# Turning the 16 by 16 corners of the attention probabilities on VectorE instead of TensorE

## The chip, the cores and the metric

The kernel runs on 1 core of a Trainium2 chip. The metric is the device time of one execution in microseconds; it is the median of several runs. Beside it stands one execution recorded by the hardware profiler. The engines are named as the profile names them: PE is TensorE's matmul, PEld its weight load, DVE is VectorE, ACT is ScalarE, POOL is GpSimd, SP is SyncE, whose queue issues nearly all transfers.

## The reference

Two layers of a decoder trunk run over 528 positions: 16 learned meta tokens and 512 real ones, 1024 wide. Each layer normalises, projects into two groups of heads, concatenates their outputs, projects back, adds, and runs a SwiGLU feed-forward block of 2816. The part that the change touches is the first head group, 8 heads of forgetting attention (FoX) of 64 columns:

```python
def attend(q_blk, c_q, q_pos, k_, v_, c_k, k_pos):
    s = jnp.einsum('bhqd,bhkd->bhqk', q_blk, k_).astype(jnp.float32) * scale
    s = s + c_q[..., :, None] - c_k[..., None, :]
    s = jnp.where(k_pos[None, :] <= q_pos[:, None], s, -jnp.inf)
    p = jax.nn.softmax(s, axis=-1)
    return jnp.einsum('bhqk,bhkd->bhqd', p.astype(v_.dtype), v_)
```

The 16 meta queries are a block of their own; the 512 real queries go in 4 blocks of 128. The other group, 4 heads of retention (RetNet), is computed chunk by chunk and is not changed. After the second layer the meta rows are dropped.

## The kernel before

All activations are held transposed, features in partitions and positions in columns. Every product is made of numbers that are split into a high and a low part (`split`, lines 126 to 128: ScalarE copies the high part into a rounded format, VectorE subtracts it from the source for the low part), and a dense product is three matmuls per weight tile (`dense_steps`, L200). The weights come through SyncE's queue as `raw` tiles and are split into `whi` and `wlo` (L176, L177).

The FoX heads go in pairs: group g (0 to 3) holds heads 2g and 2g+1, called s = 0 and 1. `fox_steps` makes the list of steps of one group. For each head and each query block b, with b = -1 for the meta queries (first layer only) and b = 0 to 3 for the real ones, there are two steps:

- `scores(s, b)` multiplies keys and queries (L487) into a PSUM tile `psa`, of which there are four, adds the mask (L493), and lets VectorE write negated logits into a probability tile and take the minimum of a row (L494, `nmax`; block 3 has two halves whose minima are joined at L499). ScalarE then exponentiates in place and sums the rows (L507). The probability tile of b = 0 to 3 is `p_tiles[b]` (in the profile `pdNone`), of 128 x 128(b+2) columns, of which the last 112 hold zeros set once per layer; that of the meta block is one of two 128 x 128 `pm` tiles.
- `turn(s, b)` stands three steps later. It turns the block's probabilities through TensorE, 128 x 128 at a time with the identity `idt` as moving operand (`transpose_into`, L398), into PSUM, up to four in one bank, and splits each bank into `pth` and `ptl`, 128 keys x 5 key blocks x 528 queries.

A query block of 128 sees 16 + 128(b+1) keys, so its last key block holds only 16 keys, and these are visible only to the block's last 16 queries: a corner of 16 by 16.

`product(s)` multiplies the values with `pth` and `ptl` (L541 for the meta queries, L549 for the rest): key block j is used for the queries from column 128 j on. After the second head of a group the rows are scaled by the reciprocals of the sums (`rows`, L512, L514, L558, L559) and split into the mix tiles `mxh`, `mxl`.

TensorE's order is the program's: `merge` and `spread` place the steps of attention and retention between the chunks of the dense products by hand. The orders of the other engines are made by a scheduler from the same program; `high_priority` moves a piece forward and `pin` keeps one in its place. `layer` (from L1207) writes out which steps lie beside which dense products: groups 0 and 1 beside the retention projections and the next group's projections, group 2 beside half of the output projection (`add_h`, L760, adds it to the residual `h`), group 3 beside retention heads 2 and 3 and the other half.

Two early uses share the names of the probability tiles: the forget gates' weights are split into a tile tagged `pth` (`gate_weights`, L346 to L348), and the first layer's first value projection keeps its weights in a tile tagged `ptl` (`own`, L441 to L443).

Of the kernel before, what the change touches and what calls it, by code (L numbers as in the profile page):

```python
# [16 lines left out]
NK = D // 128  # L17
# [15 lines left out]
GAMMA = tuple(1.0 - 2.0 ** (-5 - h) for h in range(RH))  # L33
NEG = -1.0e30
HALF = T // 2


@with_exitstack
def hybrid_kernel(ctx, tc, x_t, w_in, w_fl, w_out, w_gate, w_up, w_down, vecs, b_fg, rope, decay, mask, ident, out_t):
# [23 lines left out]
    onec = const.tile([128, 1], F32, name="onec")  # L63
    nc.vector.memset(onec, 1.0)

    p_tiles, pm_tiles, v_tiles, end_tiles, low_keys = [], [], [], [], []
    rot = {"pm": 0}


# [10 lines left out]
    def enter_att(l):  # L80
        enter("att")
        low_keys[:] = [phase["att"].tile([128, T], F32R, name=f"kl{s}") for s in range(2)]
        for s, t in enumerate(low_keys):
            (nc.gpsimd if l else nc.vector).memset(t[64 * (1 - s):64 * (2 - s)].bitcast(F32), 0.0)

        for lst, n, cols, z0 in ((p_tiles, NBLK, None, None), (v_tiles, 2, TP, T)):
            lst[:] = [phase["att"].tile([128, cols or 128 * (i + 2)], F32, name=f"pd{z0}_{i}") for i in range(n)]
            for i, t in enumerate(lst):
                z = META + 128 * (i + 1) if z0 is None else z0
                zero(l, t[:, z:z + 128 - META])  # L90
        pm_tiles[:] = [phase["att"].tile([128, 128], F32, name=f"pm{i}") for i in range(2)] if l == 0 else []
        for t in pm_tiles:
            zero(l, t)
        end_tiles[:] = [[phase["att"].tile([128, META], F32R, name=f"rs{i}{k}") for k in range(2)] for i in range(2)]
        for t in end_tiles[0] + end_tiles[1]:
            zero(l, t.bitcast(F32))

    def zero(l, t):
        (nc.gpsimd if l else nc.vector).memset(t, 0.0)
# [50 lines left out]
    def convert(j, upto=NK, pinned=False):  # L150

        if j >= len(jobs):
            return
        job = jobs[j]
        fetch(j)
        if "make" in job:
            if "w" not in job:
                n = job["n"]
                hi, lo = (wring(job["ring"] + p) for p in ("whi", "wlo"))
                job["w"] = [(NK, hi, lo)]  # L160
                job["make"](hi[:, 0:n], lo[:, 0:n])
            return
        n = job["src"].shape[1]
        if "w" not in job:
            job["w"] = [(NK, *(job["own"]() if job["own"] else
                               [wp.tile([128, NK, 128], F32R, name=i, tag=i) for i in ("whi", "wlo")]))]
            job["split"] = 0
        sub = nc.gpsimd.tensor_sub if job["pool"] else nc.vector.tensor_sub
        while job["split"] < min(n, upto):
            c0 = job["split"]  # L170
            c1 = min(n, c0 + (2 if j < 2 and c0 < 4 else 4))
            size, hi, lo = job["w"][c0 // job["w"][0][0]]
            o = c0 % size
            hi, lo = hi[:, o:o + c1 - c0], lo[:, o:o + c1 - c0]
            with tc.high_priority() if j == 5 else ExitStack():
                pin(nc.scalar.copy(hi, job["raw"][:, c0:c1]), pinned)  # L176
            pin(sub(lo, job["raw"][:, c0:c1], hi.bitcast(F32)), pinned)  # L177
            job["split"] = c1
# [74 lines left out]
    def at(tag, dt=F32R, shape=(128, T), bufs=None):  # L253
        return phase["att"].tile(list(shape), dt, name=tag, tag=tag, bufs=bufs)
# [88 lines left out]
        nc.sync.dma_start(st["wfr"], w_fl[l])  # L343

    def gate_weights(l, st, pinned=False):
        wf = st["wf"] = at("pth", shape=(128, NK, 128))  # L346
        nc.gpsimd.memset(wf.bitcast(F32), 0.0)
        split(wf[:, :, 0:FH], wf[:, :, 32:32 + FH], st["wfr"], pinned)  # L348

    def forget_gates(l, st):  # L350
        if l:
            load_gates(l, st)
            gate_weights(l, st)
        else:
            for t, src in ((bfg, b_fg), (msk, mask), (idt, ident)):
                nc.sync.dma_start(t, src)
        wf = st["wf"]
        psf = [psum_a() for _ in FULL]
        for i in range(2 * NK):
            k, part = i // 2, i % 2  # L360
            for ps, (c0, c1) in zip(psf, FULL):
                nc.tensor.matmul(ps[:, 0:c1 - c0], wf[:, k, :], st["x"][k][part][:, c0:c1],
                                 start=(i == 0), stop=(i == 2 * NK - 1))
        z = tt("z")[0:FH]
        z2 = tt("z2")[0:FH]
        for ps, (c0, c1) in zip(psf, FULL):
            with ExitStack() if l else tc.high_priority():
                nc.scalar.copy(z2[:, c0:c1], ps[32:32 + FH, 0:c1 - c0])
                nc.vector.tensor_add(z[:, c0:c1], ps[0:FH, 0:c1 - c0], z2[:, c0:c1])
        st["z"] = z  # L370
# [31 lines left out]
    def fox_dense(l, g, ly, real, st):  # L402

        QC = REAL if real else FULL
        first = l + g == 0


        def q_done(ps):
            tq = tt("tq")
            with tc.high_priority() if first else ExitStack():  # L410
                nc.vector.scalar_tensor_tensor(sv(tq, real), pv(ps, real), RSC / 8.0, sv(ly["R"], real), ALU.mult, ALU.mult)
            st["q"] = []
            for s in range(2):
                t = at(f"qs{s}")
                a0, a1 = ROWS[s]
                b0, b1 = ROWS[1 - s]
                nc.scalar.copy(sv(t, real, a0, a1), sv(tq, real, a0, a1))
                nc.vector.tensor_sub(sv(t, real, b0, b1), sv(tq, real, a0, a1), sv(t, real, a0, a1).bitcast(F32))
                st["q"].append(t)


        def k_done(ps):
            tk = tt("tq")
            nc.vector.scalar_tensor_tensor(sv(tk, False), pv(ps, False), RSC, sv(ly["R"], False), ALU.mult, ALU.mult)
            st["k"] = []
            for s in range(2):
                kh = at(f"kh{s}")
                kl = low_keys[s]
                a0, a1 = ROWS[s]
                for b0, b1 in (ROWS[s], ROWS[1 - s]):  # L430
                    nc.scalar.copy(kh[b0:b1, :], tk[a0:a1, :])
                nc.vector.tensor_sub(kl[a0:a1, :], tk[a0:a1, :], kh[a0:a1, :].bitcast(F32))
                st["k"].append((kh, kl))

        def v_done(ps):
            vt = v_tiles[0]
            for t, (c0, c1) in zip(ps, FULL):
                nc.vector.scalar_tensor_tensor(vt[:, c0:c1], t[:, 0:c1 - c0], RSC, ly["R"][:, c0:c1],
                                               ALU.mult, ALU.mult)
            st["vt"] = vt  # L440

        def own():
            t = at("ptl", shape=(128, 2, NK, 128))  # L443
            return t[:, 0], t[:, 1]

        return [dense_steps(w_in[l, 3 * g + i], [(0, lambda k: ly["x"][k], NK, c, f)], g > 0 or (i == 2 and not first), i == 2,
                            ((), (6, 6))[i] if first and i < 2 else (1, 4), own if first and i == 2 else None, ly["wait"] if first and i < 2 else None)
                for i, (c, f) in enumerate(((QC, q_done), (FULL, k_done), (FULL, v_done)))]

    def fox_steps(g, st, ly, real):  # L450
# [21 lines left out]
        def scores(s, b):  # L472
# [5 lines left out]
                st["bc"] = bc  # L478
            bc = st["bc"]
            segs = FULL if nk == T else ((0, nk),)  # L480
            pt = take(pm_tiles, "pm") if b < 0 else p_tiles[b]
            mins = []
            normalise()
            for c0, c1 in segs:
# [21 lines left out]
            pr = pt[0:nq, 0:nk]  # L506
            nc.scalar.activation(pr, pr, AF.Exp, bias=nmax[0:nq], scale=-1.0, accum_out=rsum)  # L507
            info[s, b] = pt
            if b < 0:
                info["open"] = (pr, rsum)  # L510
            elif (s, b) == todo[-1]:
                nc.vector.reciprocal(st["sums"], st["sums"])  # L512
                st["rows"] = tt("tq")
                nc.scalar.copy(st["rows"][:, 0:SEQ].rearrange("p (b s d) -> p b s d", b=NBLK, s=2),  # L514
                               st["sums"].unsqueeze(3).broadcast_to([128, NBLK, 2, 64]))
# [6 lines left out]

        def turn(s, b):
            nq, nk, q0 = span(b)
            if b == blocks[0]:
                st["pt"] = (at("pth", shape=(128, 5, T)), at("ptl", shape=(128, 5, T)))
            pth, ptl = st["pt"]
            if (s, b) == todo[-2]:
                normalise()
            for j0, n, p3 in transpose_into(info[s, b], [128 * j for j in range(b + 2)]):  # L530
                split(pth[:, j0:j0 + n, q0:q0 + nq], ptl[:, j0:j0 + n, q0:q0 + nq], p3[:, :, 0:nq])

        def product(s):
            mt, v, pt = st["mt"], st["v"][s], st["pt"]
            a0, a1 = ROWS[s]
            b0, b1 = ROWS[1 - s]
            ol = tt("ol")
# [847 lines left out]
```

## Time and profile before

| | us |
| --- | --- |
| median of 3 runs | 1283.06 (1282.85 to 1283.12) |
| the profiled execution, time | 1283.16 |
| the profiled execution, span | 1281.3 |
| first layer, attention part, by the chain | about 0 to 283 |
| feed-forward of the first layer | about 283 to 652 |
| second layer, attention part | about 652 to 905 |
| feed-forward of the second layer, end | about 905 to 1281 |

The page of the profile gives busy times and shares per engine, then the chain that ended last: from the last instruction back, at each step, to what released it. The view of groups has rows of the form "line engine operation out<-in shape xcount | busy us, mean ns of one | idle time just before them and who ended it". The timeline and the chain have "start, duration, what". Busy TensorE time is modelled, and successive matmuls overlap, so the duration of one is longer than the spacing between two.

### The profile page before, as it was taken

How to read it: one execution, taken by the hardware profiler on the slowest of the kernel's cores; microseconds unless marked ns; L12 is line 12 of the kernel's file. 1: busy time of each engine (PE TensorE's matmuls, PEld its weight loads, DVE VectorE, ACT ScalarE, POOL GpSimd, SP SyncE). 2: the span in 40 equal slices, each digit the busy share in tenths (PEclk: the TensorE clock that was granted, in tenths of full speed). 3: DMA queues.
4: the chain of work that ended last, by engine and by line, in shares of the span. 5: the costliest groups of instructions: out<-in, count | busy, mean ns of one | idle time of the engine just before them, and what ended most of it. 6: DMA issues, size and time to landing. Idle time of an engine off the chain costs nothing.

```text
span 1281.3 us, 23300 instructions
## 1 busy us (share of the span) xinstructions
PE 1264.0 (99%) x9337; PEld 1203.7 (94%) x9337; DVE 1013.4 (79%) x1826; ACT 692.2 (54%) x1248; POOL 180.8 (14%) x147
## 2 busy tenths in 40 slices
PE   9999999999999999999999999999999999999997
PEld 8899999999999999999998989899789999999996
DVE  7877856879988888887686878568899887888866
ACT  7666555676544444444455665557765444444445
POOL 2233333210000000000014334333000000000001
PEclk9999999999999999999999999999999999999999
DMA  6222222223333233332323122222223322333321
GB/s 231 76 67 84 75 85 83 65 69 116 109 97 99 99 99 99 100 99 83 100 76 116 60 99 84 75 91 67 99 79 125 111 99 99 99 100 99 100 81 66
DMA packets 45676, 120.54 MB, mean 94 GB/s; under 512 B 5360, under 2 KB 12272, under 8 KB 45568
## 3 DMA queue, kind: packets, MB, share of 16 engines
q1 hardware_dynamic: 45136, 118.77, 28.4%
q8 instruction: 73, 1.20, 0.4%
q14 instruction: 35, 0.29, 0.1%
q10 hardware_dynamic: 432, 0.29, 0.1%
HBM read 116.91 MB, written 2.13 MB: 93 GB/s over the span
## 4 chain that ended last, share of the span: by engine, by line
PE 85%; DVE 8%; ACT 3%; DMA 2%; issue 1%; DVEq 0%; SPq 0%; ACTq 0%
PE psd L200 25%; PE psa L857 18%; PE psd L992 14%; PE psd L857 13%; PE psa L992 4%; PE psa L200 4%; PE psa L398 2%; PE psa L487 1%; PE psa L549 1%; PE psa L706 1%; PE psa L676 1%; DMA raw<-w_in 1%; ACT whi L176 1%; DMA bc<-cdr 1%; DMA dec<-decay 0%
## 5 line engine op out<-in xcount | busy, mean ns | idle before, releaser
L177 POOL TENSOR_TENSOR wlo<-raw,whi 128x512 fp32r<-128x512 f32 x126 | 172.2, 1381 | 385.1 <-ACT whi L176 364.6
L200 PE MATMUL psd<-xh,whi 128*128 128x264 f32 (+1 forms) x792 | 195.7, 314 | 0.0
L200 PE MATMUL psd<-xl,whi 128*128 128x264 f32 (+1 forms) x792 | 185.9, 302 | 0.6 <-DVE xl L303 0.6
L200 PE MATMUL psd<-xh,wlo 128*128 128x264 f32 (+1 forms) x792 | 186.5, 303 | 0.0
L200 PEld LDWEIGHTS psd<-xh,wlo 128*128 128x128 f32 x792 | 126.8, 188 | 6.3 <-DVE wlo L177 0.4
L200 PEld LDWEIGHTS psd<-xh,whi 128*128 128x128 f32 x792 | 128.0, 189 | 4.7 <-ACT whi L176 0.5
L200 PEld LDWEIGHTS psd<-xl,whi 128*128 128x128 f32 x792 | 127.4, 188 | 5.1 <-DVE xl L303 1.2
L176 ACT CAST whi<-raw 128x512 fp32r<-128x512 f32 (+1 forms) x168 | 98.2, 614 | 38.6 <-PE psd L200 17.9
L845 ACT CAST whi<-raw 128x1024 fp32r<-128x1024 f32 (+2 forms) x62 | 54.9, 885 | 51.2 <-PE psd L857 38.8
L845 ACT CAST fwhi<-raw 128x1024 fp32r<-128x1024 f32 (+2 forms) x62 | 55.6, 897 | 47.5 <-PE psd L857 40.0
L846 DVE TENSOR_TENSOR wlo<-raw,whi 128x1024 fp32r<-128x1024 f32 (+2 forms) x62 | 62.9, 1014 | 12.2 <-ACT whi L845 12.1
L846 DVE TENSOR_TENSOR fwlo<-raw,fwhi 128x1024 fp32r<-128x1024 f32 (+2 forms) x62 | 63.9, 1031 | 7.9 <-ACT fwhi L845 7.8
L857 PE MATMUL psa<-th,whi 128*128 128x264 f32 (+1 forms) x232 | 65.5, 282 | 0.0
L857 PE MATMUL psa<-th,wlo 128*128 128x264 f32 (+1 forms) x232 | 65.4, 282 | 0.0
L857 PE MATMUL psa<-tl,whi 128*128 128x264 f32 (+1 forms) x232 | 65.3, 282 | 0.0
L507 ACT ACTIVATE pdNone<-pdNone,nmax 128x144 f32<-128x144 f32 (+1 forms) x64 | 36.9, 576 | 50.7 <-DVE nmax L494 33.9
L857 PE MATMUL psa<-th,fwhi 128*128 128x264 f32 (+1 forms) x224 | 63.4, 283 | 0.0
L857 PE MATMUL psa<-tl,fwhi 128*128 128x264 f32 (+1 forms) x224 | 63.3, 283 | 0.0
L857 PE MATMUL psa<-th,fwlo 128*128 128x264 f32 (+1 forms) x224 | 63.3, 282 | 0.0
L128 DVE TENSOR_TENSOR ptl<-psa,pth 128x512 fp32r<-128x512 f32 (+4 forms) x88 | 41.9, 491 | 26.9 <-ACT pth L127 26.9
L845 ACT CAST fwhi<-S 128x1024 fp32r<-128x1024 f32 x20 | 21.0, 1049 | 68.6 <-PE psa L857 66.5
L923 ACT COPY e<-psa 128x264 f32<-128x264 f32 (+1 forms) x114 | 42.8, 375 | 28.1 <-PE psa L857 23.8
(342 smaller groups left out, 4036.2 us busy)
## 6 DMA issues: line engine op xcount, KB each, us to landing
raw<-w_in SPq DMA_DIRECT2D x54, 512.0 KB, 3.5
raw<-w_gate SPq DMA_DIRECT2D x44, 512.0 KB, 4.0
fraw<-w_up SPq DMA_DIRECT2D x38, 512.0 KB, 3.4
raw<-w_down SPq DMA_DIRECT2D x64, 256.0 KB, 2.8
raw<-w_out SPq DMA_DIRECT2D x16, 512.0 KB, 3.4
raw<-w_down SPq DMA_DIRECT2D x32, 192.0 KB, 2.5
bc<-cdr SPq DMA_DIRECT2D x16, 264.0 KB, 3.3
raw<-w_up SPq DMA_DIRECT2D x6, 512.0 KB, 3.5
```

The source lines that it names most:

```text
L128: pin(nc.vector.tensor_sub(lo, src, hi.bitcast(F32)), pinned)
L176: pin(nc.scalar.copy(hi, job["raw"][:, c0:c1]), pinned)
L177: pin(sub(lo, job["raw"][:, c0:c1], hi.bitcast(F32)), pinned)
L200: nc.tensor.matmul(ps[1][b][:, 0:c1 - c0], w[:, wk, :], x[:, c0:c1], start=(k == 0 and i == 0), stop=(k == n - 1 and i == 2))
L398: nc.tensor.transpose(ps[:, 128 * j:128 * j + 128], src[:, o:o + 128], idt)
L487: nc.tensor.matmul(sc[0:nq, 0:c1 - c0], st["q"][s][:, q0:q0 + nq], kk[:, c0:c1], start=(i == 0), stop=(i == 1))
L507: nc.scalar.activation(pr, pr, AF.Exp, bias=nmax[0:nq], scale=-1.0, accum_out=rsum)
L845: nc.scalar.copy(hi, src)
L846: nc.vector.tensor_sub(lo, src, hi.bitcast(F32))
L857: nc.tensor.matmul(bank()[:, 0:b.shape[-1]], a[:, o + k, :], b, start=(fresh and k == 0 and i == 0), stop=(k == n - 1 and i == 2), skip_gr ...
L923: nc.scalar.copy(self.t["e"][:, i], self.t["x"][:, 0:w])
L992: nc.tensor.matmul(v[:, 0:c1 - c0], a[:, s * n + k, :], b[:, c0:c1], start=(k == 0 and i == 0), stop=(k == n - 1 and i == 2))
```

## The change

The four probability tiles become one tile `pr` of 128 x 1792 columns, in which block b starts at column 416 b. The corner of block b then starts at column 544 b + 128, a fixed step, so one access pattern (`ends`) reaches the four corners, 32 columns wide each: 16 keys and 16 columns of zeros. After the last block of a head is exponentiated, one VectorE instruction turns partitions 96 to 127 of all four, as four 32 by 32 blocks, into a small tile `pe`. The meta block's 16 by 16 probabilities are turned in the same way from a 32 by 32 tile. `turn` sends one key block less per query block through TensorE, and none for the meta block; the corners are split from `pe` into the probability tiles in one 16 x 4 x 16 piece at the last block. `pth` and `ptl` become tiles that last for the layer, since the columns of a corner below its 16 keys must be zero: GpSimd clears these columns once per layer (`corners`), and they stay. The forget gates' weights move to the tiles of `mxh2` and `mxl2`, and the value projection's weights to `mxh0`, `mxl0`, `mxh1`, `mxl1`, in two halves of four tiles each.

```diff
+PSTEP = 416
...
+        p_tiles[:] = [phase["att"].tile([128, PSTEP * NBLK + 128], F32, name="pr")]
+        zero(l, ends(p_tiles[0])[96:128, :, META:2 * META])
...
+        t_tiles[:] = [phase["att"].tile([128, NBLK + 1, T], F32R, name=f"pt{i}") for i in "hl"]
+        for t in t_tiles:
+            nc.gpsimd.memset(corners(t).bitcast(F32), 0.0)
+        pm_tiles[:] = [phase["att"].tile([32, 32], F32, name=f"pm{i}") for i in range(2)] if l == 0 else []
...
+    def ends(t):
+        return t.rearrange("p (n c) -> p n c", c=2 * META)[:, 4::(PSTEP + 128) // (2 * META)]
+
+    def corners(t):
+        return t.rearrange("p j c -> p (j c)").rearrange("p (n c) -> p n c", c=META)[:, ::(T + 128) // META]
...
-        wf = st["wf"] = at("pth", shape=(128, NK, 128))
-        nc.gpsimd.memset(wf.bitcast(F32), 0.0)
-        split(wf[:, :, 0:FH], wf[:, :, 32:32 + FH], st["wfr"], pinned)
+        st["wf"] = [at(f"mx{p}2", shape=(128, HB, 128)) for p in "hl"]
+        for i, wf in enumerate(st["wf"]):
+            nc.gpsimd.memset(wf.bitcast(F32), 0.0)
+            split(wf[:, :, 0:FH], wf[:, :, 32:32 + FH], st["wfr"][:, HB * i:HB * i + HB], pinned)
...
         def own():
-            t = at("ptl", shape=(128, 2, NK, 128))
-            return t[:, 0], t[:, 1]
+            return [(HB, *[at(f"mx{p}{i}", shape=(128, HB, 128)) for p in "hl"]) for i in range(2)]
...
-            pt = take(pm_tiles, "pm") if b < 0 else p_tiles[b]
+            pt = take(pm_tiles, "pm") if b < 0 else p_tiles[0][:, PSTEP * b:PSTEP * b + nk]
...
             info[s, b] = pt
+            if b == blocks[-1]:
+                st["ends"] = at("pe", F32, (32, NBLK, 32), 2)
+                nc.vector.transpose(st["ends"], ends(p_tiles[0])[96:128])
...
         def turn(s, b):
             nq, nk, q0 = span(b)
-            if b == blocks[0]:
-                st["pt"] = (at("pth", shape=(128, 5, T)), at("ptl", shape=(128, 5, T)))
-            pth, ptl = st["pt"]
+            pth, ptl = t_tiles
             if (s, b) == todo[-2]:
                 normalise()
-            for j0, n, p3 in transpose_into(info[s, b], [128 * j for j in range(b + 2)]):
+            if b < 0:
+                e = at("pe", F32, (32, NBLK, 32), 2)[:, 0]
+                nc.vector.transpose(e, info[s, b])
+                split(pth[0:META, 0, 0:META], ptl[0:META, 0, 0:META], e[0:META, 0:META])
+                return
+            for j0, n, p3 in transpose_into(info[s, b], [128 * j for j in range(b + 1)]):
                 split(pth[:, j0:j0 + n, q0:q0 + nq], ptl[:, j0:j0 + n, q0:q0 + nq], p3[:, :, 0:nq])
+            if b == blocks[-1]:
+                split(*[corners(t)[0:META, 1:] for t in (pth, ptl)], st["ends"][0:META, :, 32 - META:32])
```

More of the change, by code (lines that the diff above doesn't have):

```diff
@@ L64, in hybrid_kernel @@
     nc.vector.memset(onec, 1.0)
-    p_tiles, pm_tiles, v_tiles, end_tiles, low_keys = [], [], [], [], []
+    p_tiles, t_tiles, pm_tiles, v_tiles, end_tiles, low_keys = [], [], [], [], [], []
     rot = {"pm": 0}
@@ L84, in enter_att @@
             (nc.gpsimd if l else nc.vector).memset(t[64 * (1 - s):64 * (2 - s)].bitcast(F32), 0.0)
[L86 to L91, printed above, removed]
+        p_tiles[:] = [phase["att"].tile([128, PSTEP * NBLK + 128], F32, name="pr")]
+        zero(l, ends(p_tiles[0])[96:128, :, META:2 * META])
+        v_tiles[:] = [phase["att"].tile([128, TP], F32, name=f"pd{i}") for i in range(2)]
+        for t in v_tiles:
+            zero(l, t[:, T:TP])
+        t_tiles[:] = [phase["att"].tile([128, NBLK + 1, T], F32R, name=f"pt{i}") for i in "hl"]
+        for t in t_tiles:
+            nc.gpsimd.memset(corners(t).bitcast(F32), 0.0)
+        pm_tiles[:] = [phase["att"].tile([32, 32], F32, name=f"pm{i}") for i in range(2)] if l == 0 else []
         for t in pm_tiles:
@@ L164, in convert @@
         if "w" not in job:
-            job["w"] = [(NK, *(job["own"]() if job["own"] else
-                               [wp.tile([128, NK, 128], F32R, name=i, tag=i) for i in ("whi", "wlo")]))]
+            job["w"] = job["own"]() if job["own"] else \
+                [(NK, *[wp.tile([128, NK, 128], F32R, name=i, tag=i) for i in ("whi", "wlo")])]
             job["split"] = 0
@@ L361, in forget_gates @@
             for ps, (c0, c1) in zip(psf, FULL):
-                nc.tensor.matmul(ps[:, 0:c1 - c0], wf[:, k, :], st["x"][k][part][:, c0:c1],
+                nc.tensor.matmul(ps[:, 0:c1 - c0], wf[k // HB][:, k % HB, :], st["x"][k][part][:, c0:c1],
                                  start=(i == 0), stop=(i == 2 * NK - 1))
@@ L524, in turn @@
             nq, nk, q0 = span(b)
-            if b == blocks[0]:
-                st["pt"] = (at("pth", shape=(128, 5, T)), at("ptl", shape=(128, 5, T)))
-            pth, ptl = st["pt"]
+            pth, ptl = t_tiles
             if (s, b) == todo[-2]:
                 normalise()
-            for j0, n, p3 in transpose_into(info[s, b], [128 * j for j in range(b + 2)]):
+            if b < 0:
[4 more added lines that the diff above has]
+            for j0, n, p3 in transpose_into(info[s, b], [128 * j for j in range(b + 1)]):
                 split(pth[:, j0:j0 + n, q0:q0 + nq], ptl[:, j0:j0 + n, q0:q0 + nq], p3[:, :, 0:nq])
+            if b == blocks[-1]:
+                split(*[corners(t)[0:META, 1:] for t in (pth, ptl)], st["ends"][0:META, :, 32 - META:32])
         def product(s):
-            mt, v, pt = st["mt"], st["v"][s], st["pt"]
+            mt, v, pt = st["mt"], st["v"][s], t_tiles
             a0, a1 = ROWS[s]
```

## The prediction

> **What bounds the kernel now.** I read the page first, then what TensorE waits for.
>
> ```profile
> span 1281.3 us, 23300 instructions
> PE 1264.0 (99%) x9337; PEld 1203.7 (94%) x9337; DVE 1013.4 (79%) x1826; ACT 692.2 (54%) x1248; POOL 180.8 (14%) x147
> PE 85%; DVE 8%; ACT 3%; DMA 2%; issue 1%; DVEq 0%; SPq 0%; ACTq 0%
> ...
> PE psa L1238 <- DVE wide L60: 1.6, 1, 1.6
> PE psa L549 <- DVE ptl L128: 1.2, 1, 1.2
> ...
> PE psd L200 <- DVE h L760: 0.3, 1, 0.3
> ```
>
> TensorE is busy for 1264.0 of 1281.3 us, and it carries 85% of the chain that ended last. Its longest waits are single ones of 1.6, 1.2 and less. So an instruction taken from TensorE should shorten the run by its own time on the chain, wherever the chain is on TensorE. But 8% and 3% of the chain are on VectorE and ScalarE: there the two engines run level with TensorE, and TensorE's time is worth nothing unless theirs shrinks too. The prediction has to say how many of the removed transpositions stand in the one kind of stretch and how many in the other.
>
> **What is removed.** Today a query block b with its b+2 key blocks costs b+2 transpositions on TensorE (`turn`, L398), the last of them for 16 keys. Afterwards it costs b+1, and the block of the 16 meta queries (b = -1, in the first layer only) costs none. In the first layer that is one each from five blocks, in the second from four, for 2 heads of 4 groups: 8 x 5 + 8 x 4 = 72. The built program agrees: TensorE has 9334 matrix instructions before and 9262 after, in the same order otherwise.
>
> ```profile
> L398 PE MATMUL psa<-idt,pdNone x224: 270/272/328, 46.7 to 888.9; 128*128 128x128 f32 x112
> L398 PE MATMUL psa<-idt,pdNone 128*128 128x128 f32 x224 | 34.7, 273 | 0.0
> ...
> 42.45 0.55 PE psa L398 x5
> 43.72 0.11 PE psa L398
> 43.83 0.73 PE psd L200 x6
> 46.87 0.22 PE psa L398 x2
> 48.70 0.33 PE psa L398 x3
> 51.44 0.44 PE psa L398 x4
> ```
>
> The first row gives 272 ns from start to end of one, the second 34.7/224 = 155 ns in which no other matmul is counted. Neither is what one adds to the run, since they overlap. The chain of waits shows that: groups of 1 to 5 take 0.11, 0.22, 0.33, 0.44 and 0.55 us, so 0.11 us for each, with no fixed part. I take 0.11, because it is a spacing on the path itself. 72 x 0.11 = 7.9 us is the whole gain if nothing else moves; 72 x 0.155 = 11.2 us is the upper bound that I do not believe.
>
> [...]
>
> **Where those 72 stand.** Views: the chain in order of time, the busy time of one stretch (its columns are the stretch, its length, then busy time of PE, PEld, DVE, ACT and POOL), and three rows of the timeline.
>
> ```profile
> 52.94 0.48 ACT pth L127
> 59.30 0.61 DVE ptl L128
> 59.95 1.45 PE psa L549 x9
> ...
> 80.90 0.70 DVE mixt L559
> 155.96 0.63 DVE h L760
> 156.63 1.01 PE psd L200 x6
> ...
> 80.90:156.60 75.70, 74.34 (x606) 73.15 (x604) 61.86 (x138) 46.35 (x106) 25.37 (x18) 1.00 0.21 69
> ...
> 240.66 0.62 ACT whi L176
> 246.49 0.60 DVE mixt L553
> ...
> 712.90 0.60 ACT pth L127
> 723.40 0.70 DVE sql L128
> ...
> 54.15 0.71 PE L398 MATMUL psa<-idt,pdNone 128*128 128x128 f32 x5
> 101.00 0.27 PE L398 MATMUL psa<-idt,pm 128*128 128x128 f32 x1
> 244.26 0.33 PE L398 MATMUL psa<-idt,pm 128*128 128x128 f32 x1
> ```
>
> From 80.90 to 156.63 no step of the chain is on TensorE, although TensorE is busy for 74.34 of 75.70 us there: two engines run level, and VectorE, in its queue order, is ahead by a hair. All 10 removed transpositions of the second head group (g = 1, first layer; the first is the row at 101.00) lie in it. One more lies at 54.15, behind 52.94, where the chain goes to the split and comes back to TensorE at 59.95, and one at 244.26, between 240.66 and 247. Between 712.90 and 724 the split that the chain starts with comes after the last transposition of its head, so none is lost there. That makes 12 in level stretches and 60 on the chain: 60 x 0.11 = 6.6 us sure, 12 x 0.11 = 1.3 us that only count if VectorE gets quicker too.
>
> **What VectorE and ScalarE get.**
>
> ```profile
> L128 DVE TENSOR_TENSOR ptl<-psa,pth 128x512 fp32r<-128x512 f32 x32 | 22.0, 687 | 19.0 <-ACT pth L127 19.0
> L128 DVE TENSOR_TENSOR ptl<-psa,pth 128x384 fp32r<-128x384 f32 x16 | 8.8, 550 | 3.3 <-ACT pth L127 3.3
> L128 DVE TENSOR_TENSOR ptl<-psa,pth 128x256 fp32r<-128x256 f32 x16 | 6.6, 413 | 3.6 <-ACT pth L127 3.6
> L128 DVE TENSOR_TENSOR ptl<-psa,pth 128x128 fp32r<-128x128 f32 x16 | 4.5, 280 | 0.0
> L128 DVE TENSOR_TENSOR ptl<-psa,pth 128x16 fp32r<-128x16 f32 x8 | 1.3, 162 | 1.0 <-ACT pth L127 1.0
> L493 DVE TENSOR_TENSOR psa<-psa,msk 128x128 f32<-128x128 f32 x64 | 18.6, 291 | 8.7 <-PE psa L487 8.5
> ...
> L507 ACT ACTIVATE pdNone<-pdNone,nmax 128x528 f32<-128x528 f32 x16 | 11.8, 737 | 16.6 <-DVE nmax L499 16.6
> L507 ACT ACTIVATION_READ_ACCUMULATOR pdNone<-pdNone,nmax 128x1 f32 x64 | 12.0, 187 | 0.0
> L512 DVE RECIPROCAL sums<-sums 128x8 f32<-128x8 f32 x8 | 1.6, 197 | 2.5 <-ACT pdNone L507 2.5
> ```
>
> Per head, the splits of blocks 0, 1 and 2 lose a key block each: 413 to 280, 550 to 413, 687 to 550, together 0.41 us off VectorE (ScalarE's copies shrink alike). Block 3 keeps one piece of 512 and trades its second piece of 128 columns (0.28) for the corner split of 16 x 64, for which 128x16 at 0.16 is the nearest row. So 0.41 + 0.12 = 0.53 us is saved per head.
>
> New on VectorE is the transposition itself, four 32 x 32 blocks in one instruction: no row shows one. By its 128 columns it lies between the 128x16 row, 0.16, and the 128x128 row, 0.29; the four blocks read 128 columns, so I take 0.25. In the first layer the meta block's transposition of one 32 x 32 block joins it, 0.16 by the smallest row. So VectorE's busy time stays level: 0.53 off and 0.41 on per head in the first layer, 0.53 off and 0.25 on in the second.
>
> What is not level is the wait. The order of the built program puts the transposition of the corners into VectorE's queue behind the minimum of block 3 (`nmax`, L499), and it needs block 3's exponentials: 0.74 + 0.19 = 0.92 us on ScalarE. For a group's second head, VectorE already waits for these today, with the reciprocal of the sums (L512, 2.5 us in all). For the first head the wait is new. In five of the eight (groups 1 and 2 of the first layer, 1, 2 and 3 of the second) it stands within one short instruction of the minimum, so VectorE stands still for up to 0.9 us, with the next head's masks, score minima and splits queued behind it, and TensorE waiting for those once its four score banks are used up. Also, the meta block's transposition and split now stand ahead of the first `add_h` of the projection that follows group 1 (L760, the row at 155.96); those are some 0.16 for the transposition, 0.16 for ScalarE's copy and 0.16 for the subtraction.
>
> In the level stretch the sum is: two heads, 2 x 0.53 off; 2 x 0.41 on; one new wait of 0.9; 0.5 ahead of L760. That is up to 1.2 us later on VectorE. 75.70 - 61.86 = 13.8 us of gaps lie in that stretch and take part of it; I put the loss at 0.4 us, ends 1.2 and -0.2. Everywhere else I put 0.2 us for the other new waits, ends 0 and 2: VectorE's share is 79% and the chain stays on TensorE there.
>
> **Edits with one answer.** The weights of the forget gates and of the first value projection move from the probability tiles to mix tiles, one more short split on each engine at the start; GpSimd clears two tiles of 512 columns and two sets of corners in place of one of 1024.
>
> ```profile
> 0.73 0.95 POOL L347 MEMSET pth<- 128x1024 f32 x1 [0.29 <-POOLq L1373]
> 22.09 5.49 POOL L177 TENSOR_TENSOR wlo<-raw,whi 128x512 fp32r<-128x512 f32 x4 [20.41 <-PE psa L362]
> ...
> 641.57 0.43 SPq L1218 DMA_DIRECT2D cr<-rope  x1
> ```
>
> GpSimd is idle from there to 22.09, so that is free; without that cover it would cost one of those 0.95. SyncE's queue keeps its order. In the second layer the rope load at 641.57 gets a new wait, for a matmul 150 ahead of the layer's last; at 0.73/6 = 0.12 us each that one ends 18 us before the layer does, ahead of 641.57, so nothing comes of it. The probability tiles become persistent, so a head's first split waits for the same readers as before and no other.
>
> **The sum.** 6.6 - 0.4 - 0.2 = 6.0 us off. The profiled execution took 1283.16 us, 1.9 of it outside the span; the median of the runs is 1283.06, so both stand for each other. 1283.16 - 6.0 = 1277.2 us.
>
> **Rivals.**
>
> First, all of it: VectorE's smaller splits pull the level stretches along, and 7.9 us come off, 1275.2. For it speaks that the new waits lie where VectorE often has gaps. Against it speaks the chain between 80.90 and 156.63. Chance 0.25.
>
> Second, VectorE takes back half: the new waits reach TensorE in four of the eight first heads, 4 x 0.92 = 3.7, less the 0.6 already counted, so 6.0 - 3.1 = 2.9 off, 1280.3. For it: the second layer's first groups have the same dense mix as the level stretch, at 79% VectorE. Against it: TensorE waits there today almost nowhere. Chance 0.10.
>
> Third, slower: the wait at the head of VectorE's queue reaches TensorE for all 16 heads, with the transposition itself: 16 x (0.92 + 0.29) = 19.4 on, 7.9 off, 1294.7. It decides from seven heads on (7.9/1.21). Against it: half of these waits exist today behind L512, and cost 2.5 us of VectorE's time in all. Chance 0.05. [...]
>
> Fourth, no change: the stream on TensorE is paced by its weight loads (94%) and the removed transpositions filled gaps. Against it: the chain's groups grow by 0.11 with each one. Within 2.6 us of the old time, chance 0.07.
>
> **How the numbers follow.** Forecast 0.53, rivals 0.25, 0.10, 0.05 and 0.07. A measurement of this kernel can tell about 0.2%, 2.6 us. Faster than that: 0.53 + 0.25 + 0.10 = 0.88; same 0.07; slower 0.05. The range goes from the full 7.9 plus the 1.2 us wait at 59.95, should the shorter split remove most of it (1283.16 - 8.9 = 1274.3), to the edge of no change, 1280.5, which takes in the second rival.
>
> **What would show it.** Right: 72 fewer rows at the transposition line; groups at 0.11; the chain on TensorE from 156 on, with the time up to the start of the first layer's feed-forward some 2.5 us shorter (19 + 5 + 4 transpositions on the chain, 3.1, less 0.6), and 3.5 us shorter in the second layer's attention (32 x 0.11). VectorE's transposition at 0.16 to 0.29 us, with waits for `pr` of up to 0.9 us in front of it. Wrong: TensorE waiting over 1 us for `ptl`, `nmax` or `h` in several heads, a transposition of 0.5 us or more, or the feed-forward stretches changing length.

## The result and the profile after

The changed kernel takes 1278.79 us (median of 6 runs, 1277.50 to 1278.89), the kernel before 1282.95 us beside it (1282.61 to 1283.61): 4.2 us less, a ratio of 0.9964 with a 95% interval of 0.9953 to 0.9974. The forecast was 6.0 us less, 1277.2 us. The profiled execution took 1278.89 us. From its page, the span, the busy times and the chain:

```profile
span 1277.1 us, 23190 instructions
...
PE 1258.0 (99%) x9265; PEld 1197.8 (94%) x9265; DVE 1019.4 (80%) x1849; ACT 687.7 (54%) x1250; POOL 181.0 (14%) x150
...
PE 84%; DVE 10%; ACT 4%; DMA 1%; issue 1%; DVEq 0%; POOL 0%; ACTq 0%
```

TensorE has its 72 matmuls less and 6.0 us less busy time; VectorE has 6.0 us more, where the prediction had it level. The chain still is TensorE's, with more of VectorE in it. The transpositions that are left still stand in the chain at 0.11 us each (L409 is the old L398):

```profile
164.10 0.11 PE psa L409
...
166.55 0.22 PE psa L409 x2
...
169.19 0.33 PE psa L409 x3
...
171.96 0.44 PE psa L409 x4
```

The groups of VectorE's new work (count, busy us, mean ns of one, idle time ahead and who ended it), and below them, from the view of waits (us in total, times, longest), three waits of TensorE that are new or longer than before (1.2, none and 0.3 us):

```profile
L138 DVE TENSOR_TENSOR ptl<-pe,pth 16x64 fp32r<-16x64 f32 x16 | 6.3, 396 | 3.5 <-ACT pth L137 2.1 <-PE psa L409 1.3
...
L521 DVE STREAM_TRANSPOSE pe<-pr 32x128 f32<-32x128 f32 x16 | 4.8, 302 | 6.7 <-ACT pr L517 6.4
...
L543 DVE STREAM_TRANSPOSE pe<-pm 32x32 f32<-32x32 f32 x8 | 1.6, 197 | 0.2
```

```profile
PE psa L567 <- DVE ptl L138: 1.7, 1, 1.7
...
PE psa L409 <- DVE psa L503: 1.1, 1, 1.1
PE psd L210 <- DVE h L778: 0.9, 1, 0.9
```

To see where time came and went, the start of the same matmul in two traces is compared, along TensorE's order with the transpositions left out. For instance the output projection's matmul at 282.84 in the kernel before starts at 281.62 in the changed one, a lead of 1.22 us. This table gives "start here less start in the kernel before" for the changed kernel and for the experiments below (minus is earlier; the columns e1 to e7 are the runs e1_fill, e2_prio, e3_no_vt, e5_corners, e6_again and e7_pins):

| start before, us | what lies ahead of it | changed | e1 | e2 | e3 | e5 | e6 | e7 |
| --- | --- | --- | --- | --- | --- | --- | --- | --- |
| 56.4 | start, 5 transpositions | -1.23 | -0.13 | -1.26 | -0.98 | +0.03 | -0.58 | -1.05 |
| 68.5 | the first product | +0.37 | -0.02 | -3.19 | -1.96 | +1.84 | -2.26 | -2.98 |
| 104.9 | level stretch | -0.12 | -0.52 | -2.69 | -1.55 | +2.48 | -1.52 | -2.48 |
| 111.0 | block 3 of group 1's first head | +0.99 | +0.58 | -1.61 | -1.75 | +3.13 | -0.32 | -2.72 |
| 153.4 | the rest of group 1 | +0.32 | -0.09 | -2.28 | -2.42 | +2.57 | -0.40 | -3.26 |
| 159.4 | the first sum of the projection | +0.97 | +0.58 | -1.63 | -1.76 | +2.56 | +0.25 | -3.28 |
| 380.2 | first layer's attention | -1.15 | -1.51 | -3.67 | -3.85 | +1.09 | -0.29 | -5.35 |
| 1181.5 | second layer's attention | -4.31 | -4.69 | -6.76 | -7.29 | -1.84 | +0.15 | -8.69 |

Of the first row's 1.23 us the five transpositions make 0.55. A lead of 0.37 is there at 43.4, ahead of the first of them: TensorE's wait for `z` (L380) fell from 1.2 to 0.4 us, and one for `kl` (L443) grew from 0.2 to 0.8. No run took these two apart from the rest.

Between 159.4 and 1181.5 the changed kernel gains 5.3 us for its last 52 transpositions (0.97 + 4.31; at 0.11 each, 5.7). It loses 1.6 us across the first product, 1.1 at block 3 of group 1 and 0.65 at the first sum of the projection. The feed-forward stretches keep their length: the lead is -1.15 us at every matmul looked at from 340 to 650.

The largest loss is one that no part of the prediction had. Busy times in two windows (columns: the window, its length, busy PE, PEld, DVE, ACT, POOL, then the granted TensorE clock, DMA share and GB/s), first of the kernel before, then of the changed one:

```profile
57.50:60.95 3.45, 2.21 (x15) 1.79 (x14) 3.36 (x8) 1.52 (x4) 1.23 (x1) 1.00 0.29 85
60.95:64.40 3.45, 3.45 (x31) 3.45 (x31) 2.10 (x10) 1.37 (x4) 0.00 (x0) 1.00 0.16 67
```

```profile
57.50:60.95 3.45, 1.85 (x13) 1.80 (x14) 2.40 (x5) 1.96 (x6) 0.38 (x1) 1.00 0.43 152
60.95:64.40 3.45, 3.45 (x18) 3.45 (x17) 1.89 (x7) 0.49 (x2) 0.00 (x0) 0.51 0.02 4
```

In the second window TensorE's clock is 0.51 in place of 1.00: 18 matmuls lie in it where 31 did. Ahead of it lies the pause for `ptl`. On the timeline of the changed kernel:

```profile
56.87 0.48 PE L567 MATMUL psa<-pth,vv 128*128 128x512 f32 x1
59.10 0.51 PE L567 MATMUL psa<-ptl,vv 128*128 128x512 f32 x1 [1.75 <-DVE ptl L138]
...
61.43 0.42 PE L497 MATMUL psa<-kh,qs 128*128 128x264 f32 x1
61.65 0.42 PE L497 MATMUL psa<-kl,qs 128*128 128x264 f32 x1
```

The pause was 1.22 us and is 1.75 now: TensorE starts the product 1.40 us earlier (56.87 against 58.27), the split on VectorE only 0.86 (58.36 against 59.22). From 60.95 to 64.37, 3.41 us, the clock is 0.50, and successive 264-column matmuls stand 0.22 us apart (61.43, 61.65), where they stand 0.12 apart at full clock in the kernel before (62.16, 62.28). By an estimate from these, half speed over 3.41 us costs 1.7.

### The profile page after: what moved, and what is told of

Its sections match the earlier page's. It is cut to its first block, busy times and chain, and to the rows that moved or that the text cites. A ratio compares the mean times of both kernels' runs of the same rounds, so it can differ in the third digit from the quotient of the medians.

```text
span 1277.1 us, 23190 instructions
## 1 busy us (share of the span) xinstructions
PE 1258.0 (99%) x9265; PEld 1197.8 (94%) x9265; DVE 1019.4 (80%) x1849; ACT 687.7 (54%) x1250; POOL 181.0 (14%) x150
## 4 chain that ended last, share of the span: by engine, by line
PE 84%; DVE 10%; ACT 4%; DMA 1%; issue 1%; DVEq 0%; POOL 0%; ACTq 0%
PE psd L210 24%; PE psa L875 18%; PE psd L1010 14%; PE psd L875 13%; PE psa L1010 4%; PE psa L210 3%; PE psa L409 2%; PE psa L497 1%; PE psa L567 1%; PE psa L724 1%; PE psa L694 1%; DVE qs L429 1%; DMA bc<-cdr 1%; DVE pr L504 1%; DVE rsl L138 0%
## 5 line engine op out<-in xcount | busy, mean ns | idle before, releaser
L187 POOL TENSOR_TENSOR wlo<-raw,whi 128x512 fp32r<-128x512 f32 x126 | 172.3, 1381 | 380.2 <-ACT whi L186 380.2
L517 ACT ACTIVATE pr<-pr,nmax 128x144 f32<-128x144 f32 (+1 forms) x64 | 36.9, 576 | 42.8 <-DVE nmax L504 30.5
L1010 PE MATMUL psd<-ah,fwlo 128*128 128x264 f32 (+1 forms) x200 | 56.6, 330 | 0.0
```

The lines of the kernel that those rows point to most:

```text
L1010: nc.tensor.matmul(v[:, 0:c1 - c0], a[:, s * n + k, :], b[:, c0:c1], start=(k == 0 and i == 0), stop=(k == n - 1 and i == 2))
```

## The experiments

**Is it the clock?** The pause was filled with matmuls whose result is overwritten; nothing else moves on any engine.

```diff
             po = psum_a()
+            if g == 0 and s == 0 and not real:
+                for _ in range(6):
+                    nc.tensor.matmul(po, v[:, 0, :], pt[0][:, 0, META:T], start=True, stop=True)
             for j in range(5):
```

> The changed kernel with six extra matmuls of 128x128x512 (0.21 us each on the chain, 1.3 us together), repeats of the opening matmul of the first product in group 0 of the first layer, put into the pause in which TensorE waits 1.75 us for ptl (57.35 to 59.10); the orders of all other engines stay the same. Theory A: 1.5 to 1.7 of the 1.8 us by which the change fell short are the half clock granted from 60.95 to 64.37, which follows that pause; with the pause down to about 0.5 us the clock stays at 1.00, the mean clock of a run rises from 0.996 to 0.998, and the time falls to 1277.3 us. Theory B: the shortfall is VectorE's new instructions and waits, and the clock only happened to be there; time 1278.8 as before, or longer by what of the extra work does not fit the pause.

Measured: 1278.02 us, the kernel before beside it 1283.52; ratio 0.9954 (0.9941 to 0.9966). The same windows:

```profile
57.50:60.95 3.45, 3.07 (x18) 2.38 (x17) 3.43 (x8) 1.75 (x6) 1.29 (x1) 1.00 0.24 56
60.95:64.40 3.45, 3.45 (x30) 3.45 (x29) 2.00 (x10) 0.85 (x2) 0.00 (x0) 1.00 0.24 96
```

The clock stays at 1.00 and the second window holds 30 matmuls. Across the product this kernel loses 0.1 us (-0.13 to -0.02), the changed one 1.6, so 1.5 us come back although TensorE does more. By the times, each against the kernel before beside it, the lead grew from 4.16 us to 5.50, so 1.3 of the 1.5 expected. The profiled execution itself lost 1.1 us in the first 8 us, ahead of anything that was changed (TensorE waits 0.9 us for `whi` there, and the changed kernel doesn't). Theory A holds for the trace. Three extra matmuls do the same:

> The changed kernel with three extra matmuls in the pause ahead of the first product in place of six (0.64 us), so that 1.1 us of the 1.75 are left: about what the kernel before has (1.22). Theory A, with the half clock coming only for a pause longer than that of the kernel before: clock 1.00, 1277.3 us as with six. Rival: a pause of 1.1 us is enough once the stretch around it is thin: half clock, 1278.9 us.

Measured: 1277.73 us, ratio 0.9954 (0.9940 to 0.9967); a pause of 1.1 us, the clock 1.00 from 60 to 70, and no loss across the product (-0.90 at 56.4, -0.79 at 68.5). None of the ten runs of these two kernels has a mean clock below 0.997; six of the changed kernel's eleven runs, those below included, have 0.996. So the extra work helps through the clock.

**The pause itself taken away.** The last split of group 0 goes ahead of a rotation on both engines:

```diff
+                with tc.high_priority() if b == blocks[-1] and g == 0 and not real else ExitStack():
                     split(pth[:, j0:j0 + n, q0:q0 + nq], ptl[:, j0:j0 + n, q0:q0 + nq], p3[:, :, 0:nq])
```

> The changed kernel with the last split of a head in group 0 of the first layer put forward on ScalarE and VectorE (ahead of the rotation of a retention head, L612 and L613), so that ptl is there before TensorE asks for it. Theory A: the pause of 1.75 us at 57.35 all but goes, the clock stays at 1.00, and the time falls by 1.5 for the clock and up to 0.5 for the pause, 1276.8 to 1277.3 us. Theory B: at most the pause, 1278.3 us.

Measured: 1276.56 us, ratio 0.9943 (0.9931 to 0.9956). TensorE has no wait of its own between 50 and 70 and gains 1.9 us across the product (-1.26 to -3.19) in place of losing 1.6; 0.8 of that is given back between 80 and 99. Is this worth as much without the change?

> The kernel before, with only the last split of group 0 of the first layer put forward. Theory A: it has no half clock to lose, so only the pause of 1.22 us at 58.74 comes off, 1282.3 us (0.1% below the kernel before); the change with the same split put forward is then 5.5 to 6 us below it, the forecast of 6.0. Rival: the split put forward is worth 2.4 us in this kernel too, 1281.1 us, and the clock has no part in it.

Measured: 1283.19 us, ratio 0.9994 (0.9986 to 1.0003): 0.55 us below its kernel before, less than expected. At 62.4 it was 1.6 us ahead of where it stood at 56.4; then TensorE waits anew, by the view of waits:

```profile
PE psa L398 <- DVE mixt L554: 1.0, 1, 1.0
```

So putting the split forward is not worth 2.4 us in itself. With it in both, the change is worth 6.96 - 0.55 = 6.4 us (1283.52 - 1276.56 and 1283.74 - 1283.19).

**The pause made longer in the kernel before.** VectorE writes one piece of `ptl` twice.

```diff
+                if b == blocks[-1] and g == 0 and s == 0 and not real and j0 == 0:
+                    with tc.high_priority():
+                        nc.vector.tensor_sub(ptl[:, j0:j0 + n, q0:q0 + nq], p3[:, :, 0:nq],
+                                             pth[:, j0:j0 + n, q0:q0 + nq].bitcast(F32))
```

> The kernel before, with VectorE writing one piece of the last split of the first head (ptl, 128x512, 0.69 us) a second time with the same values, so that TensorE's pause ahead of the first product grows from 1.22 to about 2 us; nothing else changes. Theory A: a pause of that length brings the half clock for 3.4 us in this kernel too; 0.7 to 0.9 us for the pause and 1.5 to 1.7 for the clock, 2.2 to 2.6 more, 1285.9 us. Theory B, by which the half clock belongs to the change and not to the pause: the pause alone, 1284.4 us, clock 1.00 between 60 and 70.

Measured: 1284.92 us (1283.35 to 1287.45), ratio 1.0012 (1.0003 to 1.0021). The pause is 2.0 us, and theory A missed for the profiled execution: the clock was full from 60 to 70, and half elsewhere, behind a wait of 1.2 us at the start that the kernel before has too. The windows ahead of both places, each with the one that follows:

```profile
22.63:26.04 3.41, 2.01 (x13) 1.56 (x12) 1.03 (x3) 3.36 (x9) 3.28 (x3) 1.00 0.47 154
26.04:29.46 3.42, 3.42 (x18) 3.42 (x17) 3.00 (x6) 0.29 (x1) 2.18 (x2) 0.50 0.54 159
60.18:63.59 3.41, 1.83 (x13) 1.79 (x14) 2.21 (x6) 1.14 (x3) 0.00 (x0) 1.00 0.41 154
63.59:67.00 3.41, 3.41 (x31) 3.41 (x30) 2.88 (x11) 1.83 (x6) 0.00 (x0) 1.00 0.09 25
```

The second pause is the longer one and leaves TensorE the less busy (1.83 us against 2.01), and yet only the first is followed by the half clock.

Over the 11 runs the mean clock is 0.995 in three (mean 1286.6 us), 0.996 in four (1285.0) and 0.997 in four (1283.7). The kernel before shows such groups too: of its 21 runs beside e6 to e8, ten have 0.996 (mean 1284.3 us) and eight 0.998 (1283.7). So the kernel before can lose the clock as well, and whether it does changes from run to run; at which place these runs lost it is not known. The length of the pause alone doesn't decide it.

**The changed kernel again**, beside e6, e7 and e8:

> The changed kernel itself, beside the others of this group. Theory A: the pause ahead of the first product is 1.7 us or more, and most of its runs show the half clock (a mean clock of 0.996), so it stays some 4 us below the kernel before; a run that keeps the clock takes 1.3 to 1.5 us less. Theory B, by which the clock has no part: no such two groups.

Measured: 1279.16 us (1277.71 to 1280.58), ratio 0.9965 (0.9952 to 0.9977). The pause and the half clock are there again (1.7 us; 0.84 on the mean from 60 to 70). The one run with a mean clock of 0.998 took 1277.71, the others 1279.12 to 1280.58. In the first six runs it was the same: 0.998 once, 1277.50 us; 0.996 or 0.997 five times, 1278.31 to 1278.89. So without the half clock the change takes some 1277.5 us, by two runs of eleven. (3.41 us at half clock take 0.0013 off a mean clock, and the half clock at the end of a run, 6.1 us long in the trace of the kernel before and 7.8 in that of the changed one, 0.0024 and 0.0031; so 0.997 leaves it open.)

**The price on VectorE.** First without the transposition of the corners:

```diff
-                st["ends"] = at("pe", F32, (32, NBLK, 32), 2)
-                nc.vector.transpose(st["ends"], ends(p_tiles[0])[96:128])
+                st["ends"] = ends(p_tiles[0])[0:32]
...
-                split(*[corners(t)[0:META, 1:] for t in (pth, ptl)], st["ends"][0:META, :, 32 - META:32])
+                split(*[corners(t)[0:META, 1:] for t in (pth, ptl)], st["ends"][0:META, :, 0:META])
```

> The changed kernel without the 16 transpositions of the corners on VectorE: the corners are split as they lie, in the same shape, so their values are left unturned. Theory A: a transposition (0.30 us) and its wait (up to 0.9) cost time only where VectorE sets the pace, that is at 104 to 107 in group 1 of the first layer, where TensorE falls back 1.24 us; about 0.9 us comes off, 1277.9 us if the half clock stays, 1276.4 if it goes with it. Theory B: they cost in most heads, 3 us or more come off, 1275.8 us or less.

Measured: 1275.96 us, ratio 0.9937 (0.9924 to 0.9951); the half clock went (pause 0.48 us). That part goes with VectorE's order: in this kernel the scheduler put the last split of that head ahead of the rotation (56.79 and 57.39), as e2 does by hand; in the changed kernel it stands behind (58.36 and 57.36). In the table it loses nothing between 104.9 and 111.0 (-1.55 to -1.75), where the changed kernel loses 1.1. Its 32 transpositions of the second layer bring 3.4 us against 3.2. So a transposition costs time at that one place and little elsewhere, theory A. What stands there, on the timeline of the changed kernel (first VectorE's rows, then GpSimd's), and last the same minimum in the kernel before:

```profile
103.86 0.08 DVE L504 DVE_READ_ACCUMULATOR2_ANT nmax<- 128x1 f32 x1
103.98 1.27 DVE L509 TENSOR_TENSOR nmax<-nmax 128x1 f32<-128x1 f32 x1
106.14 0.30 DVE L521 STREAM_TRANSPOSE pe<-pr 32x128 f32<-32x128 f32 x1 [0.89 <-ACT pr L517]
```

```profile
102.70 2.53 POOL L187 TENSOR_TENSOR wlo<-raw,whi 128x512 fp32r<-128x512 f32 x2 [5.10 <-ACT whi L186]
```

```profile
104.67 0.16 DVE L499 TENSOR_TENSOR nmax<-nmax 128x1 f32<-128x1 f32 x1
```

The wait of 0.89 us is the predicted one. Ahead of it a minimum over one column takes 1.27 us in place of 0.16 and ends with GpSimd's two subtractions (102.70 + 2.53 = 105.23; 103.98 + 1.27 = 105.25). In e3 the minimum takes 1.27 us too and costs TensorE nothing, since the wait behind it is gone. In e5, below, it takes 0.16, and the place costs 0.65 (+2.48 to +3.13) with the wait alone. So both together make the 1.1.

Then with the meta block's transposition back on TensorE (its tile 128 x 128 again):

```diff
-                e = at("pe", F32, (32, NBLK, 32), 2)[:, 0]
-                nc.vector.transpose(e, info[s, b])
-                split(pth[0:META, 0, 0:META], ptl[0:META, 0, 0:META], e[0:META, 0:META])
+                for j0, n, p3 in transpose_into(info[s, b], [0]):
+                    split(pth[:, 0:1, 0:META], ptl[:, 0:1, 0:META], p3[:, :, 0:META])
```

> The changed kernel with the meta block turned on TensorE again (8 transpositions of 128x128), the corners still on VectorE. Theory A: 7 of the 8 are paid at 0.11 us, 0.8 us more, and the 0.63 us that TensorE loses at 156.9, behind the meta block's transposition and split ahead of the first sum of the projection, comes back: 1278.9 us, the same within the measurement. Theory B, by which VectorE's instructions are what costs: 8 x 0.6 us less on VectorE, 1 us or more off, 1277.8 us.

Measured: 1280.39 us, ratio 0.9972 (0.9961 to 0.9984), slower than either theory had it. The table says why: 1.1 us at the start as in e1, and 1.8 lost across the product, where the pause is 1.89 us and the clock halves again:

```profile
57.60:61.00 3.40, 1.51 (x10) 1.15 (x9) 3.38 (x8) 1.84 (x5) 1.27 (x1) 1.00 0.17 23
61.00:64.50 3.50, 3.50 (x18) 3.50 (x18) 0.92 (x2) 0.76 (x2) 0.00 (x0) 0.51 0.32 128
```

The disputed place is clear: between 153.4 and 159.4 nothing is lost (+2.57 to +2.56), where the changed kernel loses 0.65. There, in the changed kernel:

```profile
155.74 0.20 DVE L543 STREAM_TRANSPOSE pe<-pm 32x32 f32<-32x32 f32 x1
156.20 0.16 DVE L138 TENSOR_TENSOR ptl<-pe,pth 16x16 fp32r<-16x16 f32 x1 [0.27 <-ACT pth L137]
...
156.84 0.70 DVE L778 TENSOR_TENSOR h<-psd,h 128x528 f32<-128x528 f32 x1
```

0.20 + 0.27 + 0.16 = 0.63 us stand ahead of the sum that TensorE waits for.

**The price on TensorE.** In the kernel of e2, each query block's first transposition is done twice, 64 in all.

> The kernel with the split put forward, and 64 of the 72 removed transpositions put back on TensorE as repeats of a block's first transposition (one for each query block of 128, none for the meta block), their result overwritten; all of VectorE's new work stays. Theory A, 0.11 us each wherever TensorE sets the pace: 8 of the 64 lie in the level stretch of group 1, so 56 x 0.11 = 6.2 us more than without them, 1282.8 us. Rival, 155 ns each: 64 x 0.155 = 9.9 us more, 1286.5 us. Rival, they fill gaps of TensorE: the same, 1276.6 us.

Measured: 1283.28 us, ratio 0.9996 (0.9987 to 1.0005); against e2, 6.96 - 0.46 = 6.5 us more by the times, and 0.15 + 6.76 = 6.9 us by the traces, 0.108 us each (VectorE's order differs a little between the two). The rivals, 9.9 and 0, are out. But the eight in group 1 are paid too: from 80.7 to 159.4, e6 goes from -2.24 to +0.25 and e2 from -3.29 to -1.63, so the gap between them grows by 0.83 us, 0.10 for each, in the stretch that I had called level.

**The waits taken out of VectorE's way**, on top of e2, in the first layer:

```diff
+                info["due"] = True
+                if s or real:
+                    turn_ends()
...
+        def turn_ends():
+            if info.pop("due", False):
+                st["ends"] = at("pe", F32, (32, NBLK, 32), 2)
+                pin(nc.vector.transpose(st["ends"], ends(p_tiles[0])[96:128]), not real)
...
+            if b >= 0:
+                turn_ends()
...
-                nc.vector.transpose(e, info[s, b])
+                pin(nc.vector.transpose(e, info[s, b]), g > 0)
```

> The kernel with the split put forward, and in the first layer VectorE's transposition of the first head's corners kept behind the work that is traced before the next write of the probabilities, the meta block's transposition behind the mask and score minima of the head's first blocks. Theory A: the step of 1.2 us at 105 to 108 (wait for the exponentials of block 3 at the head of VectorE's queue) and the one of 0.63 us at 156.9 both go, 1.5 to 1.9 us off, 1274.8 us. Rival: the waits only move to the next instruction that is not ready, or the corners come too late for the product; the same, 1276.6 us, or slower.

Measured: 1274.46 us (1274.37 to 1275.41), ratio 0.9928 (0.9916 to 0.9941), 9.3 us below the kernel before. This is the fastest version. Both steps are gone (-2.48 to -2.72, -3.26 to -3.28). On its timeline the minimum is followed by work that is ready, and the transposition comes 7 us later with no wait:

```profile
102.42 0.16 DVE L511 TENSOR_TENSOR nmax<-nmax 128x1 f32<-128x1 f32 x1
102.50 0.88 DVE L671 TENSOR_REDUCE mean<-psa 128x4 f32<-128x512 f32 x2
...
109.57 0.30 DVE L536 STREAM_TRANSPOSE pe<-pr 32x128 f32<-32x128 f32 x1
```

The same in the second layer does not pay:

> The kernel with the split put forward and the first layer's transpositions kept behind, with the second layer's transposition of the first head's corners kept behind too. Theory A: the second layer loses 0.3 to 0.6 us to this wait (its 32 removed transpositions gave 3.2 of 3.5 us), so at most 0.6 us more come off, 1274.0 us. Rival: with the transposition pinned, the score minima of the next head's first block come later than now, and TensorE waits for those: 1274.5 to 1276 us.

Measured: 1275.42 us, ratio 0.9936 (0.9924 to 0.9949). Its lead falls from 6.33 to 5.24 us between 700.7 and 740.5, where e7 keeps 6.2. The time is the rival's, the mechanism only in part: the joined minimum of block 3 comes 1.9 us later than in e7 (698.37 against 696.44), but the two waits of TensorE that e7 does not have there, 0.5 and 0.2 us, are for `rsh` and `rsl` of the retention heads. And the pin did not remove the wait: the transposition still stands 0.96 us for `pr`.

## Why the prediction was right, point by point

- **What binds** and **72 x 0.11**: right. The chain is TensorE's, the groups still stand at 0.11, and e6 gives 0.108. The duration of one, 0.272 us at L398 in the kernel before, is no price where 0.11 is the spacing.
- **12 of the 72 are worth nothing in level stretches**: wrong. In e6, eight put back in group 1 cost 0.83 us. A chain that runs wholly on VectorE through a stretch where TensorE is busy for 74.34 of 75.70 us says that VectorE is ahead by a hair, not that TensorE's time is free. The other four were not tried; if they count as well, the term 6.6 should have been 7.9.
- **The transposition, 0.25 and 0.16 us**: 0.302 and 0.197, the first just over its upper row. The corner split has a median of 0.20 and a mean of 0.40, since a few take longer (1.27 at most). VectorE's busy time rose by 6.0 us: the groups of splits and transpositions add 1.7 (6.4 on; 43.2 to 38.5 off), and the rest is other instructions that took longer.
- **The new wait of 0.9 at the head of VectorE's queue, and 0.5 ahead of L760**: both there, 0.89 and 0.63, at the places named. Their sum was taken at 0.4 with an end at 1.2; TensorE lost 1.1 and 0.65. The gaps on VectorE that were to absorb part of it didn't, and the minimum of 1.27 us came on top. This is the term that was mis-sized, by some 1.3 us; the 1.2 too little for the level transpositions about cancel it, and that they cancel is luck. So the 1277.5 us without the half clock lie next to the forecast in part by luck too.
- **The wait at 59.95**: the shorter split was to remove most of it at best. It grew, and brought the half clock, 1.5 us. This step was missing: who comes earlier to a wait waits longer, and the pause of 1.75 us on TensorE had a price beyond its length. It is about the whole distance from the forecast to the result (1278.79 - 1277.2 = 1.6).
- **First layer 2.5 us shorter, second 3.5**: 1.15 and 3.2. The first lacks the 1.5 of the clock.
- **The range** held because it reached down to the edge of no change, not because the clock was thought of.
- **Rivals**: all of it, 1275.2, isn't reached by the change alone, but e7 shows that it can be. Half taken back by VectorE in four heads: it was one head and one sum. Slower: 7 heads would have had to pay, and one did; with 23 more instructions on VectorE (1849 against 1826) the kernel is 4.2 us faster. No change: out, by the interval and by e6.

## What to carry to other kernels

Price an instruction on a saturated engine by its spacing on the chain, not by its duration (0.11 against 0.272 us here; e6 gave 0.108). Then look at what that engine runs into earlier: the pause on TensorE that grew from 1.22 to 1.75 us cost itself and, in the traces of the changed kernel, half the clock (for 3.41 us, 1.5 us of time), so follow the granted clock across a pause that grows. An instruction given to VectorE cost less by its length here than by what it waited for at the head of the queue; place it behind work that is ready, as e7 does, and check what that delays, as e11 shows.

## What was not expected of the hardware

TensorE's clock was halved for 3.41 us after a thin stretch. In the changed kernel the stretch ahead of it (57.50 to 60.95) had TensorE busy for 1.85 of 3.45 us, in e5 (57.60 to 61.00) for 1.51 of 3.40, in e9 (22.63 to 26.04) for 2.01 of 3.41; the clock behind them was 0.50 (60.95 to 64.37), 0.51 (61.00 to 64.50) and 0.50 (26.04 to 29.46). With 2.21 of 3.45 in the kernel before and 3.07 in e1 it stayed at 1.00. Why the same kernel loses the clock in one run and not in another is not shown; no trace here shows a run of the changed kernel that kept it.

None of these stretches was idle from end to end: in the changed kernel the half clock came behind a pause of 1.75 us, in a stretch about half empty. It did not come every time: in e9, 1.83 of 3.41 us (60.18 to 63.59), with a pause of 2.0 us, was followed by a clock of 1.00 (63.59 to 67.00). What sets this one apart stays open.

In the changed kernel VectorE's minimum over one column took 1.27 us beside GpSimd's subtraction and ended with it (105.25 and 105.23); it took 1.27 us in e1, e2 and e3 too. In the kernel before, where the minimum starts 0.13 us ahead of the end of GpSimd's subtraction (at 104.67; 102.27 + 2.53 = 104.80), it takes 0.16, and 0.16 in e5 and e7. No run here took GpSimd's instruction away, so the cause is not shown.
